# Padded rows for the moving operands of an fp32r encoder kernel

## The chip, the cores and the metric

One Trainium2 chip, one core in use. The metric is the device time of the whole kernel in microseconds (us); lower is better. The kernel before was run three times.

## What is computed

Two layers (`DEPTH = 2`) of an encoder over 272 tokens (16 learned tokens in front of 256) of width 1,024. Of each layer, per the reference:

```
u = rms_norm(h, norm_mix_pre[l]);  proj = u @ w_in[l]
y_r = retention_branch(...) @ w_ret_o[l]
y_a = attention_branch(...) @ w_att_o[l]
mix = (sigmoid(gate_r) * y_r + sigmoid(gate_a) * y_a) @ w_mix_o[l]
h = h + rms_norm(mix, norm_mix_post[l])
u = rms_norm(h, norm_ff_pre[l])
ff = square(relu(u @ w_ff1[l])) @ w_ff2[l]
h = h + rms_norm(ff, norm_ff_post[l])
```

Output: the last 256 tokens of h. The 16 learned tokens are not needed after the second layer's keys and values.

## The kernel before, in words

Everything is kept turned, channels on the 128 partitions and tokens along a row. A weight matrix is cut in **units** of 128x1024 floats (512 KB), loaded in their order of use by SyncE's queue (`fetch`, lines 103 to 112) into one of three `raw` buffers. ScalarE rounds a unit to `wh` and VectorE computes the rest `wl = raw - wh` (`unit`, lines 114 to 128), each in one of four buffers. [...] Activations are split in the same way into a high and a low tile.

A product is the sum of high x high, high x low and low x high: three matmuls, called a **step** here, on one 128x128 block of the unit (`mm3`, lines 130 to 133). The weight block is the stationary operand (loaded before its matmul), the activation row the moving one:

```
PE.matmul(ps, ah, bh, start=first, stop=False)
PE.matmul(ps, ah, bl, start=False, stop=False)
return PE.matmul(ps, al, bh, start=False, stop=last)
```

`product` (line 141) does a unit in eight steps, k = 0 to 7; step k reads row k of the activation's two tiles, from token `c0` on. `c0` is 0 in layer 0, so a matmul has 272 columns; it is 16 in layer 1, so it has 256. The products of `v_r`, `k_a`, `v_a` and `k_r` take all 272 columns in layer 1 too. Layer 0 has 46 units of the input projection, 4 of `att_o`, 8 of `ret_o`, 8 of `mix`, 32 of `ff1` and 32 of `ff2`: 130 units, 1,040 steps. Layer 1 has the first five of these, 98 units: 14 units (112 steps) with 272 columns and 84 (672 steps) with 256. Its last weight matrix runs the other way (lines 835 to 843): there the activation is the stationary operand, in blocks of 128 tokens, and the weight unit moves, 512 columns at a time, in 128 steps.

The order on each engine is that of the program, with `issue_after` holding some work back behind a named matmul. Attention and retention, in fp32 or fp32r, are put between the steps of the projection (`fill`).

**Where the tiles lie.** Memory is handed out in pools, one behind the other. At the bottom is a scratch of 16,384 bytes a partition for dynamic DMAs, then `const`, then `big` (the slots of lines 58 to 66, each as large as its largest tile), then `ring` (`raw`, `wh`, `wl`), then small tiles. In the built program `big` begins at byte 46,656 of a partition, which is 64 modulo 256, and all of its slots have 8,704 or 4,352 bytes, both multiples of 256: every tile in it begins at 64 modulo 256. `ring` begins at byte 142,400, 64 modulo 256 as well, and every weight block of 512 bytes with it. A row of T = 272 floats has 1,088 bytes, 4 x 256 + 64. So row k of an activation begins at 64 + 64k modulo 256 in layer 0 and 64 further from token 16 on. "Place" below means this remainder: 0, 64, 128 or 192. The top of the memory in use is byte 228,384 and a few.

The moving operands of weight products are `uh` and `ul` (slots 0 and 1), `ao` (slot 5), `rh` and `rl` (7, 8), `zh` and `zl` (2, 3), `fh` (5, 8, 6, 2) and `fl` (7, 9, 10a with 10b, 3).

Of the kernel before, what the change touches and what calls it, by code (L numbers as in the profile page):

```python
# [9 lines left out]
F32 = mybir.dt.float32  # L10
F32R = mybir.dt.float32r
# [6 lines left out]
P = 128  # L18
D = 1024
KD = D // P  # L20
SEQ = 256
NM = 16
T = SEQ + NM
# [3 lines left out]
KF = FF // P  # L27
UNITS = 46 + 4 + 8 + 8 + 32 + 32
TW = 400
LAG = 4  # L30
F = [8, 9, 6, 6, 2, 7, 2, 5, 4]
BEHIND = 4
# [8 lines left out]
def encoder(ctx: ExitStack, tc: tile.TileContext, order, w, h_in, gains, dec, decm, sink, sinkm, tabs, mats, esel, masks, rel, relm, grow, out):  # L41
    nc = tc.nc
# [3 lines left out]
    def pool(name, bufs=1, **kw):  # L46
        return ctx.enter_context(tc.tile_pool(name=name, bufs=bufs, **kw))
# [3 lines left out]
    ring = pool("ring", 4)  # L51
# [3 lines left out]
    psum = pool("psum", space=PSUM)  # L55
    BANKS = {"a": 3, "s": 2, "t": 2, "o": 1}
    turn = [0]

    def slot(i, name, shape=(KD, T), dt=F32):
        return big.tile([P] + list(shape), dt, tag=f"b{i}", name=name)  # L60

    def rows(t):
        return [t[:, k] for k in range(t.shape[1])]

    def half(i, name, dt=F32):
        return rows(slot(i, name, (4, T), dt))

    def bank(tag, shape=None):
        t = psum.tile([P, 512], F32, tag=tag, name="ps_" + tag, bufs=BANKS[tag])
        if shape is None:  # L70
            return t
        n = int(np.prod(shape))
        v = t[:, :n]
        if len(shape) == 2:
            v = v.rearrange("p (a b) -> p a b", a=shape[0])
        elif len(shape) == 3:
            v = v.rearrange("p (a b c) -> p a b c", a=shape[0], b=shape[1])
        return v
# [5 lines left out]
    def f(t):  # L84
        return t.bitcast(F32)

    def stt(o, a, s, b, op0=mul, op1=mul):
        V.scalar_tensor_tensor(out=o, in0=a, scalar=s, in1=b, op0=op0, op1=op1)
# [41 lines left out]
    def mm3(ps, ah, al, bh, bl, first=True, last=True):  # L130
# [3 lines that stand above are left out]
# [7 lines left out]
    def product(x, c0, tag, *name):  # L141
        wh, wl = unit(*name)
        ps = bank(tag, [T])
        for k in range(KD):
            sl = slice(k * P, (k + 1) * P)
            ins = mm3(ps[:, c0:], wh[:, sl], wl[:, sl], x[0][:, k, c0:], x[1][:, k, c0:], k == 0, k == KD - 1)
            if k == LAG and deferred:
                with tc.issue_after(ins.ins):
# [66 lines left out]
    def square(src, c0):  # L215
        sq = two.tile([P, T], F32, tag="sq", name="sq", bufs=3)
        A.activation(sq[:, c0:], src, AF.Square)
        return sq

    def enter(l, n, c0, update):  # L220
        x = slot(0, "uh", dt=F32R), slot(1, "ul", dt=F32R)
        ss = one.tile([P, T], F32, tag="ss", name="ss")

        lag = KD if n else LAG0

        def accumulate(k):
            sq = square(h[:, k, c0:], c0)
            if k == 0:
                V.tensor_scalar(out=ss[:, c0:], in0=sq[:, c0:], scalar1=8e-6, scalar2=None, op0=add)
            else:  # L230
                V.tensor_tensor(out=ss[:, c0:], in0=ss[:, c0:], in1=sq[:, c0:], op=add)

        for k in range(KD):
            if update:
                update(k)
            gk = g[:, l, n, k:k + 1]
            A.activation(x[0][:, k, c0:], h[:, k, c0:], AF.Copy, scale=gk)  # L237
            stt(x[1][:, k, c0:], h[:, k, c0:], gk, f(x[0][:, k, c0:]), op1=sub)
            if k >= lag:
                accumulate(k - lag)  # L240
        if update and n == 0:
            for k in range(KD - lag, KD):
                accumulate(k)
        return x, ss, accumulate

    def lead():
        x = slot(0, "uh", dt=F32R), slot(1, "ul", dt=F32R)
        s8 = slot(7, "s8")
        ss = one.tile([P, T], F32, tag="ss", name="ss")
        ps = [bank("asas"[m], [T]) for m in range(4)]  # L250
        behind = {}

        def put(e, method, *args, **kw):
            if e in behind:
                with tc.issue_after(behind[e]):
                    ins = method(*args, **kw)
            else:
                ins = method(*args, **kw)
            behind[e] = ins.ins

        def squares(j):
            put("A", A.activation, s8[:, 2 * j:2 * j + 2], h[:, 2 * j:2 * j + 2], AF.Square)

        def add_squares(j):
            put("V", V.scalar_tensor_tensor, out=s8[:, 0:2], in0=s8[:, 0:2], scalar=4e-6 if j == 1 else 0.0, in1=s8[:, 2 * j:2 * j + 2], op0=add, op1=add)

        for k in range(KD):
            j, c = k // 2, slice(k % 2 * 512, k % 2 * 512 + 512)
            if k % 2 == 0:
                order.append(("lead", j))  # L270
                wh = ring.tile([P, D], F32R, tag="wh", name="wh")
                wl = ring.tile([P, D], F32R, tag="wl", name="wl")
            gk = g[:, 0, 0, k:k + 1]
            put("A", A.activation, wh[:, c], leads[j][:, c], AF.Copy)
            put("A", A.activation, x[0][:, k], h[:, k], AF.Copy, scale=gk)
            put("V", V.scalar_tensor_tensor, out=x[1][:, k], in0=h[:, k], scalar=gk, in1=f(x[0][:, k]), op0=mul, op1=sub)
            put("V", V.tensor_tensor, out=wl[:, c], in0=leads[j][:, c], in1=f(wh[:, c]), op=sub)
            if k in (3, 5, 7):
                squares((k - 3) // 2)
            if k in (6, 7):  # L280
                add_squares(k - 5)
            for m in range(4):
                o = k % 2 * 512 + m * P
                mm3(ps[m], wh[:, o:o + P], wl[:, o:o + P], x[0][:, k], x[1][:, k], k == 0, k == KD - 1)
        squares(3)
        add_squares(3)
        put("V", V.tensor_tensor, out=ss, in0=s8[:, 0], in1=s8[:, 1], op=add)
        held[len(order)] = [behind["V"]]
        return x, ss, ps
# [68 lines left out]
    for l in range(DEPTH):  # L358
        c0 = 16 * l
        if l == 0:  # L360
            u, ss, early = lead()
        else:
            u, ss, _ = enter(l, 0, 0, update)
# [124 lines left out]
            V.tensor_tensor(out=vmp[r], in0=tp[r, 256:384], in1=f(vmp[r]), op=sub)  # L488

        qk = [slot(3 + i, "qk", (2, 4, T), F32R) if i == 0 else slot(9, "qkl", (2, 4, T), F32R) for i in range(2)]  # L490
        ao = slot(5, "ao", (2, 4, T), F32R)
        ql = slot("10b", "ql", (4, T), F32R), ql1
        nc.gpsimd.memset(f(ql[0][halves[1]]), 0.0)
        gt = slot(4, "gt")
# [47 lines left out]
        def behind():  # L542
            return tc.issue_after(anchor[0])
# [119 lines left out]
        def similar(hh):  # L663
            gg, t = hh % 2, hh // 2
            tt = two.tile([P, TW], F32, tag="tt", name="tt")
            tb = two.tile([P, P], F32, tag="tb", name="tb")
# [41 lines left out]
        for hh in range(8):  # L708
            with behind():
                if hh < 7:  # L710
                    similar(hh + 1)
                retained(hh)
            fill(F[7])
            if hh == 0:
                for m in range(KD):
                    stt(gt[:, m, c0:], tg[:, m, c0:], 1.0, gt[:, m, c0:], op0=add)
                rh, rl = slot(7, "rh", dt=F32R), slot(8, "rl", dt=F32R)
            if hh % 2 and hh < 7:
                with behind():
                    meta((hh + 1) // 2)  # L720
            fill(F[6])
            with behind():
                last = normed(hh)
            fill(F[5])
# [16 lines left out]
                    mm3(ps[:, c0:], wh[:, sl], wl[:, sl], ao[:, 0, k, c0:], ao[:, 1, k, c0:], k == 0, k == 3)  # L741
                stt(tha[m][:, c0:], tha[m][:, c0:], 1.0, ps[:, c0:], op0=add)

        z = slot(2, "zh", dt=F32R), slot(3, "zl", dt=F32R)
        for m in range(KD):
            ps = proj((rh, rl), c0, wide(), "ret_o", m)
            stt(thr[:, m, c0:], thr[:, m, c0:], 1.0, ps[:, c0:], op0=add)
# [13 lines left out]
        update = leave(l, 1, c0, mixed())  # L761

        u, ss, accumulate = enter(l, 2, c0, update)
        fs, behind = [], []

# [7 lines left out]
        for m in range(KF):  # L773
            if m % KD == 0:
                a, b = ((5, 7), (8, 9), (6, 10), (2, 3))[m // KD]
                fs.append((rows(slot(a, "fh", dt=F32R)), half("10a", "fl", F32R) + half("10b", "fl", F32R) if b == 10 else rows(slot(b, "fl", dt=F32R))))
            ps = proj(u, c0, wide(), "ff1", m)
            if l == 0 and 0 <= m - SUM < KD:
                accumulate(m - SUM)
            if l == 0 and m == SUM + KD:  # L780
                e2 = one.tile([P, T], F32, tag="rb", name="e2")
                A.activation(e2, mean([ss], c0), AF.Square, scale=8e-6 ** 0.5)
            behind.append((ps, fs[-1][0][m % KD][:, c0:], fs[-1][1][m % KD][:, c0:]))
            if len(behind) > BEHIND:
                squared(*behind.pop(0))
# [84 lines left out]
def _shape_constants():  # L870
# [43 lines left out]

    r = np.arange(TW)[None, :] - 144 - np.arange(P)[:, None]
    rel = np.stack([np.maximum(r, 0), np.maximum(-r, 0)], 1).astype(np.float16)
# [64 lines left out]
```

## Time and profile before

| | |
|---|---|
| median of 3 runs | 885.78 us (885.29 to 887.2) |
| the profiled execution's own time | 887.28 us |
| span of the profiled execution | 885.5 us |
| TensorE busy (matmuls), mean granted clock | 98% of the span, 0.996 |
| VectorE, ScalarE, GpSimd busy | 68%, 63%, 6% |
| DMA | 142 MB, 161 GB/s in the mean |

The profile is of one execution. Ends of matmuls are modelled there, so a busy TensorE says little; the distance from one matmul's start to the next one's says how fast it goes. In rows of the timeline the first number is the start in us from the span's start and the second the duration. The trace gives starts to the nanosecond and the view rounds them to 10 ns; a few per cent of the matmuls can be missing from it.

### The profile page before, as it was taken

The numbers are of one execution on the slowest core, as the hardware profiler recorded it, in microseconds if no ns is written. First come the engines' busy times: TensorE is split into PE (matmuls) and PEld (weight loads), VectorE is DVE, ScalarE is ACT, GpSimd is POOL, SyncE is SP. The second block draws the span as 40 slices with busy tenths as digits, with TensorE's granted clock in tenths as the row PEclk, the third lists the DMA queues.
The fourth block names the chain that finished last, engine by engine and source line by source line (L and its number), as shares of the span: only waits on it lengthen the run. The fifth ranks groups of instructions, "written<-read, shape, count | busy, mean of one in ns | idle before, by whom it ended". The sixth has DMA issues, their size and how long they took to land.

```text
span 885.5 us, 16673 instructions
## 1 busy us (share of the span) xinstructions
PE 867.0 (98%) x6514; PEld 833.0 (94%) x6514; DVE 605.1 (68%) x1113; ACT 558.8 (63%) x1034; POOL 55.5 (6%) x113
## 2 busy tenths in 40 slices
PE   9999999999999999999999999999999999999997
PEld 8899999999989999999989999999999999998885
DVE  7789888767668555444458898888686665554543
ACT  7448887666468777444355588976755587783432
POOL 2113220000000000000000042200000000000000
PEclk9999999999999999999999999999999999999999
DMA  8544444345545555555544545443366376666661
GB/s 289 170 140 128 123 132 140 117 148 170 167 140 171 187 170 178 176 170 177 178 120 144 150 120 161 143 144 120 118 205 199 98 217 196 187 192 191 189 190 69
DMA packets 41407, 142.15 MB, mean 161 GB/s; under 512 B 5360, under 2 KB 6256, under 8 KB 41328
## 3 DMA queue, kind: packets, MB, share of 16 engines
q1 hardware_dynamic: 40896, 140.43, 52.2%
q8 instruction: 51, 0.84, 0.4%
q10 hardware_dynamic: 432, 0.66, 0.2%
q14 instruction: 28, 0.23, 0.1%
HBM read 140.02 MB, written 1.05 MB: 159 GB/s over the span
## 4 chain that ended last, share of the span: by engine, by line
PE 83%; DVE 7%; ACT 6%; issue 2%; DMA 1%; POOL 0%; SPq 0%; DVEq 0%; ACTq 0%; POOLq 0%
PE ps_a L133 13%; PE ps_a L132 13%; PE ps_a L131 13%; PE ps_s L133 5%; PE ps_s L132 5%; PE ps_s L131 5%; PE ps_t L131 4%; PE ps_t L132 4%; PE ps_t L133 4%; DVE wl L127 2%; PE ps_s L842 2%; PE ps_a L842 2%; ACT wh L126 2%; PE ps_a L841 2%; PE ps_s L841 2%
## 5 line engine op out<-in xcount | busy, mean ns | idle before, releaser
L127 DVE TENSOR_TENSOR wl<-raw,wh 128x1024 fp32r<-128x1024 f32 x256 | 312.9, 1225 | 211.2 <-ACT wh L126 209.6
L126 ACT ACTIVATE wh<-raw 128x1024 fp32r<-128x1024 f32 x256 | 270.1, 1058 | 218.2 <-PE ps_a L132 67.0
L131 PE MATMUL ps_a<-uh,wh 128*128 128x272 f32 (+1 forms) x912 | 267.3, 293 | 3.2 <-ACT uh L237 2.8
L133 PE MATMUL ps_a<-uh,wl 128*128 128x272 f32 (+1 forms) x912 | 261.7, 287 | 0.2
L132 PE MATMUL ps_a<-ul,wh 128*128 128x272 f32 (+1 forms) x912 | 261.2, 287 | 0.0
L131 PEld LDWEIGHTS ps_a<-uh,wh 128*128 128x128 f32 x912 | 172.6, 189 | 5.0 <-ACT uh L237 3.2
L132 PEld LDWEIGHTS ps_a<-ul,wh 128*128 128x128 f32 x912 | 172.5, 189 | 1.1
L133 PEld LDWEIGHTS ps_a<-uh,wl 128*128 128x128 f32 x912 | 172.5, 189 | 0.9 <-DVE wl L127 0.5
L133 PE MATMUL ps_s<-uh,wl 128*128 128x272 f32 (+1 forms) x184 | 52.6, 286 | 0.3 <-DVE wl L127 0.3
L132 PE MATMUL ps_s<-ul,wh 128*128 128x272 f32 (+1 forms) x184 | 52.5, 285 | 0.0
L131 PE MATMUL ps_s<-uh,wh 128*128 128x272 f32 (+1 forms) x184 | 52.3, 285 | 0.0
L131 PE MATMUL ps_t<-uh,wh 128*128 128x272 f32 (+1 forms) x152 | 43.6, 287 | 1.3 <-ACT uh L237 1.3
L132 PE MATMUL ps_t<-ul,wh 128*128 128x272 f32 (+1 forms) x152 | 43.6, 287 | 0.0
L133 PE MATMUL ps_t<-uh,wl 128*128 128x272 f32 (+1 forms) x152 | 43.4, 285 | 0.0
L133 PEld LDWEIGHTS ps_s<-uh,wl 128*128 128x128 f32 x184 | 34.7, 189 | 0.5 <-DVE wl L127 0.5
L131 PEld LDWEIGHTS ps_s<-uh,wh 128*128 128x128 f32 x184 | 34.7, 189 | 0.0
L132 PEld LDWEIGHTS ps_s<-ul,wh 128*128 128x128 f32 x184 | 34.6, 188 | 0.0
L131 PEld LDWEIGHTS ps_t<-uh,wh 128*128 128x128 f32 x152 | 28.7, 189 | 1.5 <-ACT uh L237 1.5
L133 PEld LDWEIGHTS ps_t<-uh,wl 128*128 128x128 f32 x152 | 28.7, 189 | 0.0
L132 PEld LDWEIGHTS ps_t<-ul,wh 128*128 128x128 f32 x152 | 28.6, 188 | 0.1
L92 DVE TENSOR_TENSOR fl<-ft,fh 128x272 fp32r<-128x272 f32 (+1 forms) x64 | 27.6, 433 | 1.0 <-ACT fh L91 0.9
L91 ACT ACTIVATE fh<-ft 128x272 fp32r<-128x272 f32 (+1 forms) x64 | 27.1, 424 | 1.7
(308 smaller groups left out, 1959.1 us busy)
## 6 DMA issues: line engine op xcount, KB each, us to landing
raw<-in_w SPq DMA_DIRECT2D x256, 512.0 KB, 3.6
leads<-in_w SPq DMA_DIRECT2D x6, 256.0 KB, 5.4
tab<-in_tabs SPq DMA_DIRECT2D x2, 544.0 KB, 6.6
h<-in_h_in SPq DMA_DIRECT2D x3, 272.0 KB, 5.3
out<-yt SPq DMA_DIRECT2D x3, 256.0 KB, 2.1
leads<-in_w ACTq DMA_DIRECT2D x2, 256.0 KB, 3.7
gj<-in_grow SPq DMA_DIRECT2D x1, 512.0 KB, 4.8
mats<-in_mats SPq DMA_DIRECT2D x1, 320.0 KB, 7.4
```

What stands on the lines that cost most here:

```text
L91: A.activation(xh, x, AF.Copy)
L92: V.tensor_tensor(out=xl, in0=x, in1=f(xh), op=sub)
L126: A.activation(wh[:, c], raw[:, c], AF.Copy)
L127: V.tensor_tensor(out=wl[:, c], in0=raw[:, c], in1=f(wh[:, c]), op=sub)
L131: PE.matmul(ps, ah, bh, start=first, stop=False)
L132: PE.matmul(ps, ah, bl, start=False, stop=False)
L133: return PE.matmul(ps, al, bh, start=False, stop=last)
L841: PE.matmul(pss[i], xh, wh[:, sl], start=kk == 0, stop=False)
L842: PE.matmul(pss[i], xh, wl[:, sl], start=False, stop=False)
```

## The change

Tiles that are a moving operand of a weight product get rows of `ROW = 320` floats, 1,280 bytes, which is 5 x 256, with the 272 tokens from float `at` of the row on. `at` is 0 for `u` in layer 0, 16 for `u` in layer 1, and 32 - c0 for all the others. A tile of 192 bytes that nothing uses is put first into the pool `ring`. The scratch of the dynamic DMAs goes from 16,384 bytes to 1,024. No instruction is added, removed or moved; only addresses and row strides differ.

```
+ROW = 320
...
+    ring.tile([P, 48], F32, name="gap", bufs=1)
...
-    def half(i, name, dt=F32):
-        return rows(slot(i, name, (4, T), dt))
+    def half(i, name):
+        return rows(slot(i, name, (4, T)))
+
+    def tokens(i, name, shape=(KD,), at=32):
+        return slot(i, name, (*shape, ROW), F32R)[..., at:at + T]
...
     def enter(l, n, c0, update):
-        x = slot(0, "uh", dt=F32R), slot(1, "ul", dt=F32R)
+        x = [tokens(i, "u" + "hl"[i], at=16 * l) for i in range(2)]
...
     def lead():
-        x = slot(0, "uh", dt=F32R), slot(1, "ul", dt=F32R)
+        x = [tokens(i, "u" + "hl"[i], at=0) for i in range(2)]
...
-        ao = slot(5, "ao", (2, 4, T), F32R)
+        ao = tokens(5, "ao", (2, 4), 32 - c0)
...
-                rh, rl = slot(7, "rh", dt=F32R), slot(8, "rl", dt=F32R)
+                rh, rl = tokens(7, "rh", at=32 - c0), tokens(8, "rl", at=32 - c0)
...
-        z = slot(2, "zh", dt=F32R), slot(3, "zl", dt=F32R)
+        z = tokens(2, "zh", at=32 - c0), tokens(3, "zl", at=32 - c0)
...
-                fs.append((rows(slot(a, "fh", dt=F32R)), half("10a", "fl", F32R) + half("10b", "fl", F32R) if b == 10 else rows(slot(b, "fl", dt=F32R))))
+                low = [tokens(i, "fl", (4,), 32 - c0) for i in ("10a", "10b")] if b == 10 else [tokens(b, "fl", at=32 - c0)]
+                fs.append((rows(tokens(a, "fh", at=32 - c0)), sum(map(rows, low), [])))
...
-    nc = _bacc.Bacc("TRN2", target_bir_lowering=False, num_devices=1)
+    nc = _bacc.Bacc("TRN2", target_bir_lowering=False, num_devices=1, dynamic_dma_scratch_size=1024)
```

## Rows read from the trace of the kernel before

**Rows 1.** Page, sections 1 and 2: busy time, and the granted clock by slices.
```profile
PE 867.0 (98%) x6514; PEld 833.0 (94%) x6514; DVE 605.1 (68%) x1113; ACT 558.8 (63%) x1034; POOL 55.5 (6%) x113
...
PEclk9999999999999999999999999999999999999999
```

**Rows 2.** Page, section 4: shares of the chain that ended last.
```profile
PE 83%; DVE 7%; ACT 6%; issue 2%; DMA 1%; POOL 0%; SPq 0%; DVEq 0%; ACTq 0%; POOLq 0%
```

**Rows 3.** Waits of PE: waiter <- releaser: us in total, times, longest (first and last).
```profile
PE ps_a L131 <- ACT uh L237: 2.8, 2, 1.4
...
PE ps_s L133 <- DVE wl L127: 0.3, 1, 0.3
```

**Rows 4.** Timeline, PE, layer 0's ff2: first and last step, and one of 64 rounds between.
```profile
358.48 0.29 PE L131 MATMUL ps_s<-fh,wh 128*128 128x272 f32 x1
...
414.48 0.29 PE L131 MATMUL ps_t<-fh,wh 128*128 128x272 f32 x1
...
414.86 0.29 PE L131 MATMUL ps_t<-fh,wh 128*128 128x272 f32 x1
...
415.23 0.29 PE L131 MATMUL ps_t<-fh,wh 128*128 128x272 f32 x1
...
415.62 0.29 PE L131 MATMUL ps_t<-fh,wh 128*128 128x272 f32 x1
...
415.99 0.29 PE L131 MATMUL ps_t<-fh,wh 128*128 128x272 f32 x1
...
454.96 0.29 PE L131 MATMUL ps_s<-fh,wh 128*128 128x272 f32 x1
```

**Rows 5.** Timeline, PE, layer 1's mix: first and last step, and one of 16 rounds.
```profile
669.15 0.28 PE L131 MATMUL ps_a<-zh,wh 128*128 128x256 f32 x1
...
679.09 0.28 PE L131 MATMUL ps_a<-zh,wh 128*128 128x256 f32 x1
...
679.44 0.28 PE L131 MATMUL ps_a<-zh,wh 128*128 128x256 f32 x1
...
679.80 0.28 PE L131 MATMUL ps_a<-zh,wh 128*128 128x256 f32 x1
...
680.16 0.28 PE L131 MATMUL ps_a<-zh,wh 128*128 128x256 f32 x1
...
680.51 0.28 PE L131 MATMUL ps_s<-zh,wh 128*128 128x256 f32 x1
...
691.52 0.28 PE L131 MATMUL ps_a<-zh,wh 128*128 128x256 f32 x1
```

**Rows 6.** Timeline, PE, last matrix of layer 1: first and last of its 128 steps.
```profile
789.82 0.48 PE L841 MATMUL ps_s<-wh,fh 128*128 128x512 f32 x1
...
878.17 0.40 PE L841 MATMUL ps_a<-wh,fh 128*128 128x512 f32 x1
```

[...]

**Rows 8.** Timeline, PE and its weight loads, in layer 1's mix.
```profile
679.21 0.28 PE L132 MATMUL ps_a<-zl,wh 128*128 128x256 f32 x1
679.21 0.19 PEld L133 LDWEIGHTS ps_a<-zh,wl 128*128 128x128 f32 x1
```

**Rows 9.** Timeline, PE: retention scores, stationary at place 0, moving at place 192.
```profile
158.35 0.29 PE L675 MATMUL ps_s<-qk,qkl 128*128 128x272 f32 x1
...
158.84 0.39 PE L686 MATMUL ps_t<-sd,vr 128*128 128x272 f32 x1
```

**Rows 10.** Page, section 3: DMA queues, packets, MB, share of the 16 engines.
```profile
q1 hardware_dynamic: 40896, 140.43, 52.2%
...
q10 hardware_dynamic: 432, 0.66, 0.2%
```

**Rows 11.** Page, section 5: the split of the weight units on ScalarE and VectorE.
```profile
L127 DVE TENSOR_TENSOR wl<-raw,wh 128x1024 fp32r<-128x1024 f32 x256 | 312.9, 1225 | 211.2 <-ACT wh L126 209.6
L126 ACT ACTIVATE wh<-raw 128x1024 fp32r<-128x1024 f32 x256 | 270.1, 1058 | 218.2 <-PE ps_a L132 67.0
```

## The prediction

> **What bounds the kernel.** [...] The chain that ended last runs through TensorE for 83% [rows 2], and what TensorE waits for sums to a few us: 2.8 us for its worst releaser, 0.3 us for the weight rests `wl` [rows 3]. So the time is the number of matmuls by the distance between their starts. Of the 6,514 entries, 5,472 belong to weight products (1,824 steps of three). The rest is attention, norms and the last matrix.
>
> That distance is then read from the timeline, in stretches without a wait. In layer 0's ff2 the first and the last of 256 steps start at 358.48 and 454.96 us [rows 4]: 96.48 us / 255 = 378.3 ns a step, 126.1 ns a matmul of 272 columns. [...]
>
> **Does the place show?** Yes, a little. In layer 0's ff2 rows begin at places 64, 128, 192 and 0 in turn (k = 0 to 3), and the steps differ: rows 4 show starts at 414.48, 414.86, 415.23, 415.62 and 415.99, so about 0.38, 0.37, 0.39, 0.37 us. Over all 64 rounds of the stage the means are 381.7 (place 64), 374.2 (128), 382.5 (192) and 375.0 (0) ns, the same within a nanosecond from round to round. For 256 columns, in the 16 rounds of [rows 5], they are 352.6 (128), 355.8 (192), 357.6 (0) and 354.0 (64). So the whole spread between places is 8 ns a step for 272 columns, 5 ns for 256.
>
> What is it about the place? Two readings fit these rows equally. By the **place reading** only the row's own place counts. By the **distance reading** what counts is the row's place minus the place of the weight block, since the load of the next weights starts with the matmul, both at 679.21 in [rows 8], and two reads then run through the same memory. Before, weights are always at 64, so the two can't be told apart there. Two other rows speak for the distance. In the last matrix the moving operand stays at 64 while the stationary one goes through the places, and the 32 steps at each still differ, 698.0 (stationary at 0), 696.6 (64), 692.9 (128), 695.4 ns (192), in the stretch of [rows 6]: the stationary place matters. And the retention scores have pairs with the stationary at 0 and the moving at 192: four starts from 158.35 to 158.84 [rows 9], about 123 ns each, as quick as the good places, though the row's own place 192 is a bad one in [rows 4].
>
> **The change, part by part.**
>
> Addresses after it. Nine slots grow by 8 x 48 x 4 = 1,536 bytes and two by 768: 15,360 bytes, which is what the scratch gives up. `big` moves down by 15,360 = 60 x 256 and its slots are multiples of 256, so tiles still begin at 64; `ring` begins at the same byte as before plus 192, so weights go from place 64 to 0. Rows of 1,280 bytes keep one place: `u` of layer 0 at 64, `u` of layer 1 at 64 + 64 = 128 for its 272-column products and 192 for the others, all else at 64 + 128 = 192. Distances: 64 for `u` of layer 0, 128 for the 14 wide units of layer 1, 192 for the rest. Before, distance 64 was place 128, distance 128 place 192, distance 192 place 0.
>
> The sum by the distance reading, each against the mean step:
> - layer 0, `u`: 78 units x 8 = 624 steps x (374.2 - 378.3) = -2.6 us;
> - layer 0, the other 52 units: 416 steps x (375.0 - 378.3) = -1.4 us;
> - layer 1, wide: 112 steps x (382.5 - 378.3) = +0.5 us;
> - layer 1, narrow: 672 steps. By distance 357.6, by place 355.8, against 355.1. No row decides for 256 columns, so I take the middle, 356.7: +1.1 us (between +0.5 and +1.7);
> - last matrix: moving at 0, stationary at 192, distance 64, which was 698.0: 128 x 2.3 = +0.3 us, or -0.0 by the stationary's own place: +0.1.
>
> Together -2.3 us. No row shows a long run at one place, or weights at 0 under a weight product, so the bounds are far: above, every product at the worst step seen (382.5 and 357.6), 1,152 x 4.2 + 672 x 2.5 = +6.5 us; below, the overhead that doesn't grow with the columns. [...] 5,472 x 3 = -16 us is the lower end.
>
> [...]
>
> `raw` at place 0: loads may land sooner, but TensorE's wait for `wl`, which hangs on the loads, is 0.3 us in all [rows 3], so at most that is gained: 0. The split of a unit, 1,058 ns on ScalarE and 1,225 on VectorE [rows 11], is over 1.6 us short of the 3.0 us (8 x 378 ns) that its products take; both run ahead, and a step shorter by 4 ns takes nothing from that. Writes of activations go a row at a time, so a longer stride costs nothing. If this cover were gone, the next late thing would be `wl`, at 2.3 us a unit in sequence.
>
> Against its own 887.28 us this execution becomes 885.0; it is 1.5 us above the median of the runs, so the forecast on the median is 885.78 - 2.3 = **883.5 us**.
>
> **The rivals.**
>
> *Slower, the place reading.* Place and price: the weight products at 64 and 192, the slow places of [rows 4]. 624 x (381.7 - 378.3) + 416 x (382.5 - 378.3) = +3.9 us, layer 1 -0.5 + 0.5, last matrix 0: 889.7 us. It decides if the 272-column steps go above 378 ns. For it: the simplest reading of [rows 4]; against it: [rows 6, 9]. The same time comes out if the 192 bytes don't shift the weights: then distances are 0 and 128, both slow. So "the change doesn't do what it says" is inside this case.
>
> *No change.* The differences of [rows 4, 5] could come from the turn from one place to the next and cancel over a round; a constant place would then give the mean step, 885.8 us. For it: in [rows 4, 5] each step is followed by one at another place, so what looks like a property of a place may be one of the turn from it. [...]
>
> *A larger gain.* The turn of places itself costs, each change upsetting a stream that would otherwise settle. Price: up to the -16 us above, about half of it if only a part goes: 870 to 878 us. [...]
>
> **How the numbers follow.** Distance reading 0.37, no change 0.22, place reading 0.24, larger gain 0.17. About 0.2%, 1.8 us, is what a measurement of this kernel can tell from no change. The forecast's 2.3 us lies just beyond that, so of its 0.37 some 0.07 go to "same", and 0.01 of the larger gain; of no change 0.02 go to "slower", for layer 1. Faster 0.30 + 0.16 = 0.46; same 0.20 + 0.08 = 0.28; slower 0.24 + 0.02 = 0.26. The range takes in the first three cases with the spread of layer 1's term (881 to 891 us) and the gain case down to three quarters of its price, 874: 874 to 891. The distance case alone is 882 to 885.
>
> **What would show it.** In the changed trace each step of layer 0's ff2 should repeat with one length, not four: 375 ns by distance, 382 by place, 378 with no effect, under 370 in the larger gain; `u` products of layer 0 at 374. Layer 1's mix should have steps of 356 to 358 ns, so it pays back a part; if it falls below 353 the forecast is too cautious. Waits of TensorE, granted clock and the busy times of ScalarE and VectorE should stay as they are. The forecast is wrong if steps in layer 0 are as long as before or longer, or if the time moves with unchanged steps.

## The result, and the profile after

The changed kernel takes 876.03 us in the median of four runs (874.73 to 876.55) against 885.53 for the kernel before: a ratio of 0.9888, 95% interval 0.987 to 0.9905. That is 9.5 us less. The forecast was 2.3 us less, so the direction held, and the time lies in the range, but the gain is four times the forecast. Single runs of one kernel spread too: 19 runs of the kernel before, beside the first experiments, lie between 885.26 and 887.98 us.

The profiled execution has a span of 874.2 us after 885.5, 11.3 us less (the one shown before was the longest of its four runs). Its page, sections 1 and 4, where [rows 1] and [rows 2] stood:

```profile
PE 855.0 (98%) x6514; PEld 821.9 (94%) x6514; DVE 604.2 (69%) x1113; ACT 558.6 (64%) x1034; POOL 57.7 (7%) x113
...
PE 81%; DVE 10%; ACT 6%; issue 1%; POOL 1%; DMA 0%; DVEq 0%; ACTq 0%; POOLq 0%; SPq 0%
```

The same instructions, the same work on VectorE and ScalarE, 12 us less on TensorE. VectorE has gone from 7 to 10% of the chain; the rise lies in layer 1's projection (below).

The timeline of TensorE shows where it went. First and last step of layer 0's ff2 (256 steps), of layer 1's mix (64) and of the last matrix (128), in the changed kernel, where [rows 4], [rows 5] and [rows 6] stood (the step's first line is now L136, the last matrix's L847):

```profile
356.43 0.29 PE L136 MATMUL ps_s<-fh,wh 128*128 128x272 f32 x1
...
450.78 0.28 PE L136 MATMUL ps_s<-fh,wh 128*128 128x272 f32 x1
...
663.26 0.28 PE L136 MATMUL ps_a<-zh,wh 128*128 128x256 f32 x1
...
684.68 0.28 PE L136 MATMUL ps_a<-zh,wh 128*128 128x256 f32 x1
...
779.54 0.48 PE L847 MATMUL ps_s<-wh,fh 128*128 128x512 f32 x1
...
866.85 0.39 PE L847 MATMUL ps_a<-wh,fh 128*128 128x512 f32 x1
```

That is 94.35 us / 255 = 370.0 ns a step (378.3 before), 21.42 / 63 = 340.0 (before, 22.37 / 63 = 355.1) and 87.31 / 127 = 687.5 (before, 88.35 / 127 = 695.7). Inside ff2 the round of four lengths is gone: all but three of the 255 steps took 369 or 371 ns, all at place 192. In layer 0's ff1, whose rows are at 64, 230 of the 234 steps that can be read took 380 ns. By the terms of the sum, with the length measured in stretches without a wait:

| products | steps | ns a step, before, after | us forecast | us by the measured length |
|---|---|---|---|---|
| layer 0, u (place 64) | 624 | 378.3, 380.0 | -2.6 | +1.1 |
| layer 0, the rest (192) | 416 | 378.3, 370.0 | -1.4 | -3.5 |
| layer 1, wide (128) | 112 | 378.3, 380 | +0.5 | +0.2 |
| layer 1, narrow (192) | 672 | 355.1, 340.0 | +1.1 | -10.1 |
| last matrix | 128 | 695.7, 687.5 | +0.1 | -1.0 |

These sum to -13.3 us; the span shrank by 11.3. The last column is steps times a length, not a time measured, and not every stage gained what it has there. Taken from the first step of a stage to the first of the next, layer 1's ff1 gave 3.4 us of 3.9, and layer 1's projection 0.5 us (174.40 to 173.89) of the 3.7 that its 256 narrow and 112 wide steps have in the table. Layer 0's projection became shorter (189.71 to 188.80), where longer steps should have cost 0.6; a second profiled execution of the change has 190.16, so that is spread between executions.

In layer 1's projection attention's small matmuls stand between the products. Its narrow steps took 353.2 ns before and 342.4 after in the mean, less of a change than in the table, and part of that came back as waits. Here is the first part of this stage, from the first to the last of its wide steps, before and after: the length of the stretch, then busy time of PE, PEld, VectorE, ScalarE and GpSimd.

```profile
460.34:567.00 106.66, 104.93 (x845) 101.47 (x846) 95.58 (x226) 75.57 (x165) 20.85 (x38) 1.00 0.46 136
...
456.15:563.16 107.01, 104.49 (x845) 100.63 (x846) 95.60 (x226) 75.13 (x165) 22.87 (x38) 1.00 0.44 135
```

It got no shorter, though 120 of its steps have 256 columns. VectorE is busy for about 90% of it, and in these 110 us (460 to 570 before, 456 to 566 after) the share of the chain that goes through the rests `wl` rose from 2.4 to 14.3%: the shorter steps run into VectorE here. Waits of PE in the changed kernel, where [rows 3] stood:

```profile
PE ps_a L136 <- ACT uh L242: 2.8, 2, 1.4
PE ps_s L430 <- POOL pads L427: 2.6, 4, 0.8
...
PE ps_s L680 <- DVE tmx L93: 1.2, 1, 1.2
...
PE ps_s L138 <- DVE wl L132: 0.3, 1, 0.3
```

GpSimd's `pads` held TensorE for 2.6 us (2.0 before) and VectorE's `tmx` for 1.2 (0.7 before); the wait for `wl` is still 0.3. Not all of the 2 us has a single name in this list.

### The profile page after: what moved, and what is told of

It is laid out like the page before. It is cut to its first block, busy times and chain, and to the rows that moved or that the text cites. A ratio compares the mean times of both kernels' runs of the same rounds, so it can differ in the third digit from the quotient of the medians.

```text
span 874.2 us, 16673 instructions
## 1 busy us (share of the span) xinstructions
PE 855.0 (98%) x6514; PEld 821.9 (94%) x6514; DVE 604.2 (69%) x1113; ACT 558.6 (64%) x1034; POOL 57.7 (7%) x113
## 4 chain that ended last, share of the span: by engine, by line
PE 81%; DVE 10%; ACT 6%; issue 1%; POOL 1%; DMA 0%; DVEq 0%; ACTq 0%; POOLq 0%; SPq 0%
PE ps_a L136 12%; PE ps_a L137 12%; PE ps_a L138 12%; PE ps_s L136 5%; PE ps_s L137 5%; PE ps_s L138 5%; PE ps_t L136 4%; PE ps_t L137 4%; PE ps_t L138 4%; DVE wl L132 3%; PE ps_s L848 2%; PE ps_a L848 2%; PE ps_s L847 2%; PE ps_a L847 2%; PE ps_a L849 2%; PE ps_s L849 2%
## 5 line engine op out<-in xcount | busy, mean ns | idle before, releaser
L136 PE MATMUL ps_a<-uh,wh 128*128 128x272 f32 (+1 forms) x912 | 266.0, 292 | 2.8 <-ACT uh L242 2.8
L136 PEld LDWEIGHTS ps_a<-uh,wh 128*128 128x128 f32 x912 | 171.8, 188 | 4.4 <-ACT uh L242 3.2
L136 PE MATMUL ps_s<-uh,wh 128*128 128x272 f32 (+1 forms) x184 | 52.3, 285 | 0.0
L136 PE MATMUL ps_t<-uh,wh 128*128 128x272 f32 (+1 forms) x152 | 43.4, 285 | 1.3 <-ACT uh L242 1.3
L136 PEld LDWEIGHTS ps_s<-uh,wh 128*128 128x128 f32 x184 | 34.9, 189 | 0.0
L136 PEld LDWEIGHTS ps_t<-uh,wh 128*128 128x128 f32 x152 | 28.5, 188 | 1.5 <-ACT uh L242 1.5
```

## The experiments

The theories: **distance** (the moving row's place minus the weight block's), **place** (the row's alone), **turn** (that the place changes from step to step costs). The kernel before can't separate them. Each diff is against the changed kernel unless it says otherwise.

**Weights back at place 64.**

```
-    ring.tile([P, 48], F32, name="gap", bufs=1)
```

> The changed kernel without the unused 192 bytes: weights back at place 64, moving rows as in the change (192; 64 for u of layer 0; 128 for the wide products of layer 1). Distance theory: the rows at 192 are now 128 away from the weights, as the wide products of layer 1 were in the changed kernel (380 ns a step), so layer 0's ff2 goes from 370 to about 380 ns and layer 1's mix from 340 to about 355; 416 x 10 + 672 x 15 = +14 us, the kernel is back near 888 us. Place theory (only the row's own place counts) and turn theory (only that the place stays the same counts): nothing changes, 876 us, ff2 370 ns, mix 340 ns.

Measured: 887.7 us, ratio to the kernel before 1.0012 (1.0002 to 1.0021). The whole gain is gone. Layer 0's ff2 and layer 1's mix, first and last step:

```profile
358.24 0.28 PE L135 MATMUL ps_s<-fh,wh 128*128 128x272 f32 x1
...
455.12 0.29 PE L135 MATMUL ps_s<-fh,wh 128*128 128x272 f32 x1
...
669.34 0.28 PE L135 MATMUL ps_a<-zh,wh 128*128 128x256 f32 x1
...
691.77 0.28 PE L135 MATMUL ps_a<-zh,wh 128*128 128x256 f32 x1
```

96.88 / 255 = 379.9 ns and 22.43 / 63 = 356.0 ns: what the distance theory said. The rows lie as in the changed kernel, all 1,280 bytes apart; 192 unused bytes somewhere else decide whether they are worth 9.5 us or nothing. Place alone and turn alone fall. This run also has the padded rows and the small scratch; together they bring nothing.

**The 192 bytes alone, in the kernel before.**

```
     turn = [0]
+    ring.tile([P, 48], F32, name="gap", bufs=1)
```

> The kernel before with the unused 192 bytes alone: weights at place 0, rows of 1,088 bytes, so that the moving place still turns through 64, 128, 192 and 0. Turn theory: as before, 885.5 us, 378 and 355 ns a step in the mean. Theory that the pair of places counts (moving and weights) with no part for the turn: the steps at 192 take 370 ns in layer 0's ff2 and 340 in layer 1's mix, those at 64 and 128 about 380 in ff2; by a quarter of the steps at 192 the gain is about a quarter of 1,040 x 8 + 672 x 15 ns = 18 us, some 4 us, if the other places are as before: 881 us.

Measured: 887.08 us, ratio 1.0005 (0.9996 to 1.0014): no change. A round of four steps in layer 0's ff2, rows at 0, 64, 128, 192 and 0 again:

```profile
359.87 0.29 PE L132 MATMUL ps_s<-fh,wh 128*128 128x272 f32 x1
...
360.25 0.29 PE L132 MATMUL ps_s<-fh,wh 128*128 128x272 f32 x1
...
360.62 0.29 PE L132 MATMUL ps_s<-fh,wh 128*128 128x272 f32 x1
...
361.01 0.29 PE L132 MATMUL ps_s<-fh,wh 128*128 128x272 f32 x1
...
361.38 0.29 PE L132 MATMUL ps_s<-fh,wh 128*128 128x272 f32 x1
```

The means in this stage are 381.7 (place 0), 374.1 (64), 382.5 (128) and 375.0 (192): the four lengths of [rows 4], each moved by one place, exactly as the weights were. So the distance is what orders them. But the step at 192 takes 375 ns here and 370 in the changed kernel, with 256 columns 357 and 340. My expectation (370 and 340) missed that: the turn has a part in it. Both edits are needed, and neither does anything alone.

**u of layer 0 at 192 too.**

```
-        x = [tokens(i, "u" + "hl"[i], at=16 * l) for i in range(2)]
+        x = [tokens(i, "u" + "hl"[i], at=32 - 16 * l) for i in range(2)]
...
-        x = [tokens(i, "u" + "hl"[i], at=0) for i in range(2)]
+        x = [tokens(i, "u" + "hl"[i], at=32) for i in range(2)]
```

> The changed kernel with u of layer 0 (projection and ff1, 624 steps) at float 32 of its rows instead of 0, so at place 192 like the rest. Pair theory, in either form: its steps go from 380 to 370 ns, 624 x 10 = 6 us, the kernel takes about 870 us. Rival: these steps are long for a reason of their own (they run beside attention, or in another slot), and the kernel stays at 876 us.

Measured: 875.11 us in the median of four runs, but they lie at 870.06, 875.10, 875.11 and 876.98. In the profiled one (875.1) layer 0's u steps take 370 ns, as expected; in exchange layer 1's ff1, whose addresses are those of the changed kernel, takes 353 instead of 340:

```profile
696.11 0.28 PE L136 MATMUL ps_s<-uh,wh 128*128 128x256 f32 x1
...
776.67 0.28 PE L136 MATMUL ps_s<-uh,wh 128*128 128x256 f32 x1
```

80.56 / 228 = 353.3 ns. So there is a second length at the same addresses, and it needed runs of its own.

**The change again, and this one again, more often.** No edit.

> The change itself once more. In the kernel with u of layer 0 moved to 192 the steps of layer 1's ff1 (240 of them) took 353 ns instead of 340 in the profiled run, though their addresses are those of the change; the change of length came at the end of layer 1's mix and then stayed. If the stream has two lengths at the same addresses and falls into one or the other by small differences of time, single runs of the change should now and then be 240 x 13 = 3 us or 672 x 13 = 9 us longer than 876 us. If the history of the program decides, the runs of the change all stay within 1.5 us of 876.

> The kernel with u of layer 0 at 192 once more, more often. Two lengths by chance: runs fall into groups near 870 us (340 ns in layer 1's ff1) and 875 us or more (353 ns). One length fixed by the program: all runs near 875 us, and the one of 870 us was an exception of another kind.

Measured side by side: the change 876.08 us (0.9875 to 0.991 of the kernel before, six runs from 874.43 to 879.08); u at 192 as well 871.23 us (ratio 0.9843, 0.9821 to 0.9865, five runs: 870.37, 870.67, 871.23, 872.74 and 875.62). Here the intervals don't touch, and moving u of layer 0 is worth nearly 5 us; the first four runs of each kernel lay only 0.9 us apart, with intervals that overlap. By the steps it is 624 x 10 ns = 6.2 us. The five runs are not the two clean groups that were expected: four lie within 2.4 us and one apart.

The profiled execution of the change was one of the long ones (878.01 us). Its layer 1 mix:

```profile
664.49 0.28 PE L136 MATMUL ps_a<-zh,wh 128*128 128x256 f32 x1
...
686.75 0.28 PE L136 MATMUL ps_a<-zh,wh 128*128 128x256 f32 x1
```

22.26 / 63 = 353.3 ns. In this execution most steps were 340 ns up to 632.15 us, with runs of up to five at 353 between attention's matmuls; there two steps of `att_o` were held up (787 and 457 ns), and from the next one on all took 353 or 354, through ret_o and mix. After the pause for the norm they were soon at 340 again. In the other profiled execution of the change the same two steps were held up (789 and 457 ns) and 340 went on. In the first run with u at 192 the jump came at the norm before ff1.

So in these traces, with 256 columns at distance 192, the stream has two lengths (340 and 353 ns), keeps the one it has as long as nothing interrupts it, and may take the other after an interruption. Which one is not set by the program's addresses; what sets it wasn't found. By size it is 151 steps x 13.3 ns = 2.0 us in this execution and 3.0 us for the 228 steps of ff1. That it makes the whole spread of the runs (874.4 to 879.1 for the change) isn't shown: one execution of each has a trace, the profiled one of u at 192 took 872.74 us with ff1, ret_o and mix at 340 while others took 870.4, and the runs of the kernel before spread as well.

**All rows at place 0.** `at` is 16 larger than in the change for every tile but u of layer 0, which has 48.

```
-        x = [tokens(i, "u" + "hl"[i], at=16 * l) for i in range(2)]
+        x = [tokens(i, "u" + "hl"[i], at=(48, 32)[l]) for i in range(2)]
...
-        ao = tokens(5, "ao", (2, 4), 32 - c0)
+        ao = tokens(5, "ao", (2, 4), (48, 32)[l])
```

> The changed kernel with all rows one place on: 0 for every product from token c0 on, 192 for the wide products of layer 1; weights at 0, distance 0. If 192 with weights at 0 is a place by itself good, steps here go to about 380 ns in layer 0 and about 355 in layer 1 (about 890 us), and the wide products of layer 1 alone go to 370. By the turn theory steps stay at 370 and 340. By the order of the kernel before (place 0: 375 ns for 272 columns, 358 for 256) layer 0 would lie between and layer 1 be slow.

Measured: 883.84 us (one run). ff2 and mix:

```profile
355.77 0.29 PE L136 MATMUL ps_s<-fh,wh 128*128 128x272 f32 x1
...
451.65 0.29 PE L136 MATMUL ps_s<-fh,wh 128*128 128x272 f32 x1
...
666.08 0.28 PE L136 MATMUL ps_a<-zh,wh 128*128 128x256 f32 x1
...
688.76 0.28 PE L136 MATMUL ps_a<-zh,wh 128*128 128x256 f32 x1
```

376.0 and 360.0 ns: not 380 and 355, and not 370 and 340. A place held constant can be worse than the turn (360 against 355 with 256 columns). The wide products of layer 1, now at 192, go to 371. The last matrix, moving at 0 over a stationary at 0, went to 681 ns a step, its best in any trace.

**No address, but all distances, as in the kernel with u at 192.** All rows at place 0 as above, and the 192 bytes taken away, so that weights are at 64; u of layer 0 at distance 192 like the rest.

```
-    ring.tile([P, 48], F32, name="gap", bufs=1)
...
-        ao = tokens(5, "ao", (2, 4), 32 - c0)
+        ao = tokens(5, "ao", (2, 4), (48, 32)[l])
```

> Weights back at place 64 (no unused 192 bytes) and all rows at place 0 from token c0 on, u of layer 0 too; wide products of layer 1 at 192. No row or weight block is at the place that it has in the kernel with u of layer 0 at 192, but the distances are the same: 192, and 128 for the wide products. Distance theory: 370 ns for 272 columns, 340 (or the longer 353) for 256, about 871 us. Place theory, by the run with rows at 0 and weights at 0: 376 and 360 ns, about 884 us.

Measured: 873.5 us, ratio 0.9863 (0.9848 to 0.9878).

```profile
352.62 0.29 PE L135 MATMUL ps_s<-fh,wh 128*128 128x272 f32 x1
...
446.97 0.28 PE L135 MATMUL ps_s<-fh,wh 128*128 128x272 f32 x1
...
658.89 0.28 PE L135 MATMUL ps_a<-zh,wh 128*128 128x256 f32 x1
...
680.31 0.28 PE L135 MATMUL ps_a<-zh,wh 128*128 128x256 f32 x1
```

370.0 and 340.0 ns. Rows at the very place that gave 376 and 360 with weights at 0 give 370 and 340 with weights at 64. The distance theory stands. (This execution took 871.61 us, the shortest of the four, with part of layer 1's retention at 353; why the others took 2 to 3 us more, no trace shows.)

**Finer places.**

```
+        x = [tokens(i, "u" + "hl"[i], at=(40, 48)[l]) for i in range(2)]
...
+        ao = tokens(5, "ao", (2, 4), (24, 24)[l])
```

> The changed kernel with other places, to fill the table of lengths by distance (weights at 0): u of layer 0 at 224, the rest of layer 0 at 160, u of layer 1 at 64 from token c0 on, the rest of layer 1 at 224. Theory that the distance acts in blocks of 64 bytes: 224 behaves like 192 (370 ns for 272 columns, 340 for 256) and 160 like 128 (380 ns). Theory that it acts smoothly: 224 lies between 192 and 0 (370 and 376 for 272 columns, 340 and 360 for 256), 160 between 128 and 192 (380 and 370). u of layer 1 at 64 with 256 columns has no measured neighbour: 355 ns, the mean step, if nothing is special about it.

(40 in `lead`; `rh`, `rl`, `z` and `fs` as `ao`.) The second run has `(36, 8)[l]` for u, 36 in `lead`, and `(28, 20)[l]` for the rest:

> As the run before it with places 16 bytes off the multiples of 64 or 32: u of layer 0 at 208, the rest of layer 0 at 176, u of layer 1 at 160, the rest of layer 1 at 208. Blocks of 64 bytes: 208 like 192 (370 and 340 ns), 160 and 176 like 128 (380 for 272 columns, 355 for 256). Smooth: 208 within 2 ns of 192, 176 too, and 160 of layer 1 between 355 and 340.

Measured: 883.18 and 887.85 us (one run each). Layer 0's ff2 at 160, in the first:

```profile
356.78 0.29 PE L136 MATMUL ps_s<-fh,wh 128*128 128x272 f32 x1
...
451.14 0.29 PE L136 MATMUL ps_s<-fh,wh 128*128 128x272 f32 x1
```

94.36 / 255 = 370.0 ns at 160, though 176 gives 380, and 208 too. Neither blocks of 64 bytes nor a smooth curve: both theories missed. All lengths at a constant distance, in ns a step, each the mean of a stretch with no wait. At 192 nearly all steps are within 2 ns of a length given here; at other distances they can go through several, at 128 with 256 columns from 352 to 360.

| distance | 272 columns | 256 columns |
|---|---|---|
| 0 | 376 | 360 |
| 64 | 380 | 353 |
| 128 | 380 | 356 |
| 160 | 370 | 352 |
| 176 | 380 | - |
| 192 | 370 | 340 or 353 |
| 208 | 380 | 357 |
| 224 | 376 | 355 |
| turning | 378 | 355 |

**The last matrix at distance 192.** Against the kernel with u of layer 0 at 192; `at` of fh and fl in layer 1 alone:

```
-                fs.append((rows(tokens(a, "fh", at=32 - c0)), sum(map(rows, low), [])))
+                fs.append((rows(tokens(a, "fh", at=(32, 48)[l])), sum(map(rows, low), [])))
```

> The kernel with u of layer 0 at 192, and layer 1's fh and fl one place further (64 instead of 192). These tiles are read by the last matrix alone, as the stationary operand under 512 moving columns that begin at place 0, so the distance there goes from 64 to 192. Constant distances measured so far in that stage: 64 gives 687 ns a step, 0 gives 680, 128 gives 697. If 192 is good there as for 256 and 272 columns, a step falls below 680; by the same 10 ns a matmul as the shorter ones it would be 128 steps x 20 ns or more, 2.5 us: 868.7 us in the median, against 871.2. [...]

Measured: 873.92 us, ratio 0.9871 (0.9849 to 0.9893).

```profile
775.80 0.48 PE L847 MATMUL ps_s<-wh,fh 128*128 128x512 f32 x1
...
864.78 0.40 PE L847 MATMUL ps_a<-wh,fh 128*128 128x512 f32 x1
```

88.98 / 127 = 700.6 ns, after 687.5 at distance 64: the expectation missed. With 512 columns the order by distance is another: 0 (681), 64 (687.5), 128 (698), 192 (701). The two runs of finer places, where this distance is 32 and 48, have 700.6 as well. Distance 192, which gave the shortest steps with 256 columns, gave the longest with 512.

## Why the prediction was right, and where it was not

What bounds the kernel held in the main: TensorE's distance between starts, at a mean granted clock of 0.996 before and 0.998 after. The cover of the splits, though, did not hold everywhere. I had both splitting engines "run ahead", by a unit's split against its products (1,225 ns in 3.0 us), without the other work that VectorE has between the splits. The wait for `wl` did stay at 0.3 us; but the first part of layer 1's projection, where VectorE is busy for 90%, takes 105.6 to 107.0 us in all twelve traces, whatever the step. The share of its chain that goes through `wl` is 2 to 5% where narrow steps take 355 to 360 ns (the kernel before, the gap alone, weights at 64, rows at 0) and 13 to 14% where they take 340; with 352 and 353, in the runs of finer places, it is 2 and 18%. Of the 1.8 us that its 120 narrow steps were worth (x 15.1 ns) about 0.4 came: 106.3 us in the mean of those four traces, 105.9 in the six with 340. That a faster split would free the rest was not tested.

That rows 4 and 5 show something about place, and that it is the distance to the weight block rather than the row's own place, held too: the last matrix and the four retention scores [rows 6, 9] pointed the right way, and two runs bear it out by moving weights alone (379.9 and 356.0 ns in ff2 and mix) and weights and rows together (370.0 and 340.0). The small scratch, together with the padded rows, brought nothing (887.7 us, ratio 1.0012), nor did `raw` at 0 (887.08 us, 1.0005); in the changed kernel a load of `raw` landed in 3.7 us in the median, after 3.6. The longer stride cost nothing, as said: a row of `fh` took 424 ns in the mean before and after, one of `fl` 433 and 432.

The step that failed is the price: "the sum by the distance reading, each against the mean step" took each distance's length from steps that turn from place to place, and used it for steps that stay. Those are different numbers. With 256 columns 192 gave 357.6 ns in the turn, and I forecast +1.1 us for layer 1's narrow products; constant it gave 340, -10.1 us. With 272 columns 64 gave 374.2 in the turn and 380 when constant, so layer 0's u lost 1.1 us instead of gaining 2.6. The order of the distances isn't even the same. The table's mis-sized terms nearly all come from this. The two terms with the most steps, 1,296 of 1,824, even had the wrong sign, so that the direction of the total came out right is in good part luck.

The lower bound of -16 us, from which the range's 874 and the price of "a larger gain" come, takes 3 ns from each of 5,472 matmuls, and no run shows that term. The runs show, at a constant distance of 192, 5.0 ns less a matmul with 256 columns (118.4 to 113.3) and 2.8 less with 272 (126.1 to 123.3), and at 64 0.6 more with 272 (126.7).

The rivals: the place reading fell with the first and the last of the distance runs. "No change" would have been right if only one of the two edits had been made. "A larger gain" had the time (870 to 878 us) and partly the reason: a constant place does take away a cost, but only at some distances (340 ns after 355.1 with 256 columns at 192), and at others it adds one (360 at 0). The last matrix, whose moving place was constant before too, says nothing against it: there the stationary place turned, so the distance did, and its steps took 692.9 to 698.0 ns.

Of the signs I gave, the first is the one that showed it: one length in layer 0's ff2, 370 ns, a value between "375 by distance" and "under 370 in the larger gain". Layer 1's mix fell to 340, below the 353 at which the forecast was to be "too cautious". And one sign spoke against it: 624 of layer 0's 1,040 steps became longer (380 ns after 378.3).

The ground given for the distance reading was that the load of the next weights and the running matmul read the same memory. The runs show that where the weight block begins relative to the moving row is worth 20 ns in a step of 360 with 256 columns (340 at distance 192, 360 at 0). Whether the two reads meet in memory, or something else ties them, no run here shows.

## What to carry to other kernels

In an fp32r product that keeps TensorE full (98% busy here), measure the distance between matmul starts in stretches without a wait, and try the start of moving rows against the start of weight blocks, modulo 256 (the only remainder varied here), with rows padded so that it stays the same in every step; here a matmul of 256 columns went from 118.4 to 113.3 ns by it. Try it for each number of columns by itself, in runs, because lengths read from the kernel whose rows turn did not carry over (at distance 192 with 256 columns 357.6 ns in the turn, 340 constant). Here distance 192 was best for 256 columns, best together with 160 for 272, and among the worst for 512, and u of layer 0 moved there as well made the kernel with the lowest median, 871.23 us in five runs (875.11 in four others). Before counting a gain, look at each stage by itself: in layer 1's projection, where VectorE is busy for about 90% of the first part, shorter steps bought 0.5 us of the 3.7 that the table has.

## What was not expected

- Two lengths at the same addresses: 340 or 353 ns a step with 256 columns at distance 192, kept over stretches of 151 and 228 steps and changed only where something came between. In a trace it is worth 2 to 3 us.
- The two edits are worth nothing alone (1.0012 and 1.0005 of the time before) and 1.1% together.
- At 340 ns a step a matmul of 256 columns takes 113.3 ns, after 118.4, and no distance tried gave less; with 272 columns none gave less than 123.3 (370 a step).
- With 272 columns, 16 bytes of distance are worth 10 ns a step (160 against 176, 192 against 208).
